# Mixer order in a two-layer hybrid decoder: the third output-gate block is multiplied ahead of the last part of the linear attention

## Chip, cores and metric

The kernel runs on one core of a Trainium2 chip. The metric is the device time in microseconds of one execution, and the number quoted is the median of several runs. Beside the runs there is one execution recorded by the hardware profiler, from which all rows below come. TensorE is called PE here (its weight loads PEld), VectorE DVE, ScalarE ACT, GpSimd POOL, and SyncE, which issues the DMAs, SP.

## What is computed

Two decoder layers over 512 prompt tokens and 8 x 4 sample tokens, width 1024. Each layer has four residual sub-layers:

```
x += 0.5 * SwiGLU_1(rmsnorm(x))
h  = rmsnorm(x);  z = h @ w_in          # one projection, columns split among head groups
     A: sliding-window attention (window 128, 8 query heads, 2 key/value heads, sinks, rotary)
     B: gated linear attention (4 heads, 64 x 128 state), then per head
        o = rms_norm(o, gain) * silu(gate)
x += concat(A, B) @ w_out
x += CrossAttn(rmsnorm(x), memory K/V)
x += 0.5 * SwiGLU_2(rmsnorm(x))
```

The outputs are the new activations, caches and states. The change lies in the second sub-layer, the mixer: `gate` has four heads of 128 columns, and one block of the kernel multiplies one head.

## The kernel before

Activations lie transposed, 128 features by 544 tokens a tile (N = 544, halves of 272). A 1024-deep product of one 128-column block is made in three terms from high and low parts of weights and activations (`product`, L221): 8 x 3 weight tiles times two halves, 48 matmuls on line L230. `weights` (L209) turns a loaded slab (`raw`, three buffers) into `hi` (ACT, L213, three buffers) and `lo` (DVE, L214, two buffers).

The mixer (L679) is written as steps, generators that are cut into parts at each `yield`. The text MIX (L53) names the steps in the order in which their parts are traced; the first mention of a step runs its first part, the next mention its second, and so on (`run`, L72). From this order a planner makes each engine's instruction list: it places an instruction when its inputs and its buffer are there, and prefers what stands earlier in MIX. So an instruction that is late in MIX can come early on its engine when earlier ones can't be placed. On the chip the lists are fixed.

Buffers come from rings: `pm` in PSUM holds two tiles (for a product or for one set of scores), `pa` in PSUM four, `z` six, `s` (scores) five, `u` three.

The steps that matter here:
- `rot i` (L965): a block of the attention's keys (i = 0) or queries. ACT's `taken` (L406) reads the product twice: L409 scales it, L410 squares it into a `u` buffer. The second part rotates it, with four small DMAs into a `z` tile and DVE products L986 to L988.
- `gla n` (L817): the linear attention for 128 tokens. Part one: scores and state updates (L825, L837, L848). Part two: outputs into two `pa` banks (L861, L871). Part three, `normed` (L792): squares L799 and root L803 on ACT, reciprocal L804 and products L807 on DVE into a `z` tile, four transposes L812 on PE, gain L813 on ACT. `glas` does the same for the sample tokens; `states` (L932) makes their new states in four parts (kdm L941 and update L952 on DVE, matmuls L946).
- `qf` (L993): row sums (L272) of the four `u` tiles of the queries, copies L275, transposes L278, then the softmax factors.
- `score n w` (L538): part one multiplies scores into a `pm` tile (L554) and copies them to an `s` tile with the mask (L559/L560, or L564 on ACT and L565 on DVE). Part two: maximum L570, exponentials L576, division L584. Part three: transposes L588 and masks L592. `vals n` multiplies with the values (L604). `swas` does the sample tokens; L619 copies their queries.
- `sv`: the values of the attention, with transposes L1007 to L1011 and 18 small stores.
- `gated h` (L1022): part one takes a `z` tile, multiplies the gate block of head h (48 matmuls) and scales it from PSUM into `z` (L388 on DVE). Part two: silu L1026 on ACT and the product L1027 with the linear attention's output on DVE.
- `bparts` splits the gated outputs into high and low parts; `out half q` multiplies with `w_out` (half 1 takes group B's output, half 0 the attention's).

Of the kernel before, what the change touches and what calls it, by code (L numbers as in the profile page):

```python
# [53 lines left out]
    "rot 0, gate, key 0, query 1, value 2, query 0, key 1, qdecay 1, value 3, kdecay 1, value 3, kdecay 1, kdecay "  # L54
    "0, sv, value 2, value 0, rot 0, kdecay 0, qdecay 0, value 1, value 0, value 1, gla 0, gla 1, glas, gla 0, "
    "gla 1, gla 2, rot 1, gla 0, gla 2, glas, rot 2, gla 1, gated 0, gla 3, rot 2, rot 1, rot 3, gla 2, rot 4, "
    "glas, states, rot 3, gla 3, rot 4, gla 3, qf, qf, score 1 0, states, score 0 0, gated 0, sv, score 1 0, "
# [1454 lines left out]
```

## Time and profile before

| | before |
|---|---|
| median of 3 runs | 2189.59 us (2189.1 to 2192.12) |
| the profiled execution | 2186.67 us |
| its span, first to last instruction | 2184.5 us |
| PE busy | 2161.6 us |
| DVE busy | 1567.0 us |
| ACT busy | 1048.6 us |
| mean granted clock of PE | 0.998 |

Busy time is the time in which at least one instruction of the engine runs. The idle time of an engine is put before the instruction that ended it, with what that instruction waited for. Times in rows are microseconds from the start of the span. The mixer of the first layer lies at about 400 to 620 us, that of the second at about 1480 to 1700 us.

### The profile page before, as it was taken

How to read it: one execution, taken by the hardware profiler on the slowest of the kernel's cores; microseconds unless marked ns; L12 is line 12 of the kernel's file. 1: busy time of each engine (PE TensorE's matmuls, PEld its weight loads, DVE VectorE, ACT ScalarE, POOL GpSimd, SP SyncE). 2: the span in 40 equal slices, each digit the busy share in tenths (PEclk: the TensorE clock that was granted, in tenths of full speed). 3: DMA queues.
4: the chain of work that ended last, by engine and by line, in shares of the span. 5: the costliest groups of instructions: out<-in, count | busy, mean ns of one | idle time of the engine just before them, and what ended most of it. 6: DMA issues, size and time to landing. Idle time of an engine off the chain costs nothing.

```text
span 2184.5 us, 40867 instructions
## 1 busy us (share of the span) xinstructions
PE 2161.6 (99%) x17306; PEld 2088.7 (96%) x17306; DVE 1567.0 (72%) x2471; ACT 1048.6 (48%) x1721; POOL 7.0 (0%) x17
## 2 busy tenths in 40 slices
PE   9999999999999999999999999999999999999999
PEld 9899999997897999999999999999879979999999
DVE  7887876546764798777689777765477458977774
ACT  6444543536455644444364444445455566444441
POOL 0000000000000000000000000000000000000000
PEclk9999999999999999999999999999999999999999
DMA  4233333232335233233232322333223533233332
GB/s 151 89 104 93 113 105 121 88 92 75 96 127 202 78 107 106 87 104 101 68 106 88 107 97 88 101 126 97 77 82 98 190 131 104 94 105 93 87 107 71
DMA packets 74998, 227.07 MB, mean 104 GB/s; under 512 B 7712, under 2 KB 19744, under 8 KB 73504
## 3 DMA queue, kind: packets, MB, share of 16 engines
q1 hardware_dynamic: 74816, 224.47, 32.2%
q8 instruction: 135, 2.21, 0.4%
q14 instruction: 47, 0.39, 0.1%
HBM read 214.64 MB, written 9.04 MB: 102 GB/s over the span
## 4 chain that ended last, share of the span: by engine, by line
PE 94%; DVE 3%; DMA 1%; ACT 1%; issue 0%; SPq 0%; ACTq 0%; DVEq 0%
PE pm L230 47%; PE pa L459 36%; PE pm L1150 1%; PE pm L1112 1%; PE pa L230 1%; DMA raw<-in_wts_dram 1%; PE pm L1235 1%; PE pa L1252 1%; PE pa L604 0%; PE pa L239 0%; PE pm L554 0%; PE pa L1282 0%; PE pa L272 0%; DVE big L219 0%; PE pa L588 0%; DMA out_dram<-state 0%
## 5 line engine op out<-in xcount | busy, mean ns | idle before, releaser
L230 PE MATMUL pm<-big,hi 128*128 128x272 f32 x5632 | 780.5, 290 | 5.7 <-DVE big L316 1.9
L230 PEld LDWEIGHTS pm<-big,hi 128*128 128x128 f32 x5632 | 732.6, 188 | 15.0 <-DVE big L316 2.9
L230 PE MATMUL pm<-big,lo 128*128 128x272 f32 x2816 | 410.1, 289 | 0.0
L230 PEld LDWEIGHTS pm<-big,lo 128*128 128x128 f32 x2816 | 374.1, 188 | 2.2 <-issue 1.2
L213 ACT CAST hi<-raw 128x1024 fp32r<-128x1024 f32 x196 | 205.6, 1049 | 243.4 <-PE pm L230 132.6
L214 DVE TENSOR_TENSOR lo<-raw,hi 128x1024 fp32r<-128x1024 f32 x196 | 238.5, 1217 | 53.9 <-PE pm L230 32.0
L218 ACT CAST hs<-sum 128x1024 fp32r<-128x1024 f32 x152 | 160.0, 1052 | 172.0 <-PE pa L459 122.5
L459 PE MATMUL pa<-t,hs 128*128 128x272 f32 x1368 | 238.9, 288 | 1.3 <-ACT t L218 1.3
L459 PE MATMUL pa<-big,hs 128*128 128x272 f32 x1064 | 211.0, 288 | 2.1 <-DVE big L219 2.1
L459 PEld LDWEIGHTS pa<-t,hs 128*128 128x128 f32 x1368 | 200.9, 188 | 1.5 <-ACT t L218 1.5
L219 DVE TENSOR_TENSOR ls<-sum,hs 128x1024 fp32r<-128x1024 f32 x152 | 185.1, 1218 | 3.3 <-ACT hs L218 2.3
L459 PE MATMUL pa<-big,hi 128*128 128x272 f32 x1216 | 178.5, 289 | 0.0
L399 DVE SCALAR_TENSOR_TENSOR x<-pm,x 128x544 f32<-128x544 f32 x192 | 137.9, 719 | 47.9 <-PE pm L230 47.9
L459 PEld LDWEIGHTS pa<-big,hs 128*128 128x128 f32 x1064 | 166.3, 188 | 2.6 <-DVE big L219 2.6
L459 PEld LDWEIGHTS pa<-big,hi 128*128 128x128 f32 x1216 | 162.9, 188 | 0.0
L459 PE MATMUL pa<-t,ls 128*128 128x272 f32 x912 | 153.1, 289 | 0.0
L459 PEld LDWEIGHTS pa<-t,ls 128*128 128x128 f32 x912 | 129.7, 188 | 0.0
L218 ACT CAST hi<-raw 128x1024 fp32r<-128x1024 f32 x76 | 80.1, 1054 | 84.3 <-PE pm L230 78.2
L218 ACT CAST hd<-raw 128x512 fp32r<-128x512 f32 x76 | 47.2, 621 | 136.1 <-PE pa L459 127.3
L445 DVE TENSOR_TENSOR sum<-raw 128x512 f32<-128x512 f32 x152 | 98.2, 686 | 17.7 <-DMA raw<-in_wts_dram 17.4
L459 PE MATMUL pa<-big,lo 128*128 128x272 f32 x608 | 109.1, 288 | 0.0
L484 DVE TENSOR_TENSOR z<-pa,e 128x272 f32<-128x272 f32 x76 | 33.5, 441 | 98.2 <-PE pa L459 91.8
(306 smaller groups left out, 2675.1 us busy)
## 6 DMA issues: line engine op xcount, KB each, us to landing
raw<-in_wts_dram SPq DMA_DIRECT2D x348, 512.0 KB
big<-in_cmk_t_dram SPq DMA_DIRECT2D x8, 1024.0 KB
big<-in_cmv_dram SPq DMA_DIRECT2D x8, 1024.0 KB
kc<-in_consts_dram SPq DMA_DIRECT2D x2, 1546.0 KB
x<-in_x_dram SPq DMA_DIRECT2D x8, 272.0 KB
z<-big SPq DMA_DIRECT2D x32, 68.0 KB
out_dram<-x SPq DMA_DIRECT2D x8, 272.0 KB
cache<-in_s_dram SPq DMA_DIRECT2D x8, 256.0 KB
```

Source lines behind the costliest of these rows:

```text
L213: act.copy(out=hi, in_=raw)
L214: dve.tensor_tensor(out=lo, in0=raw, in1=hi.bitcast(F32), op=ALU.subtract)
L218: act.copy(out=hi, in_=src)
L219: dve.tensor_tensor(out=lo, in0=src, in1=hi.bitcast(F32), op=ALU.subtract)
L230: pe.matmul(half_of(ps, h, s.stop - s.start), w, x[:, s], start=i == 0, stop=i == len(steps) - 1)
L399: dve.scalar_tensor_tensor(out=x, in0=p, scalar=scale, in1=x, op0=ALU.mult, op1=ALU.add)
L445: dve.tensor_tensor(out=t[:, e], in0=t[:, 0] if x is None else x, in1=y, op=ALU.add)
L459: pe.matmul(ps, u, v, start=first and i == 0, stop=i == len(steps) - 1, skip_group_check=not first)
L484: dve.tensor_tensor(out=t[:, 1], in0=q, in1=e2, op=ALU.add)
L1112: pe.matmul(pk[:, h, :], w[:, o:o + 128], x[:, k, :], start=st and h % 2 == 0, stop=sp and h % 2 == 1)
L1150: pe.matmul(pv[:, c, :], x[:, k, c * 128:c * 128 + 128], w[:, o], start=st, stop=sp)
L1235: pe.matmul(ps[:, h, :], qn[:, h, 128 * n:128 * n + 128], held["mk"][:, h, :], start=True, stop=True)
```

## The change

In MIX, the first mention of `gated 2` moves from behind the third part of `score 1 0` to a place between the second part of `rot 4` and the third part of `gla 3`. The second mention of `gated 2` (silu and product) stays, and so does the order of all other steps. No function is changed. The order of the steps that load weights stays too: `rot 4`, `gated 2`, `gated 1`, `gated 3`.

```diff
-    "glas, states, rot 3, gla 3, rot 4, gla 3, qf, qf, score 1 0, states, score 0 0, gated 0, sv, score 1 0, "
-    "states, score 0 1, score 1 1, score 1 0, gated 2, score 0 0, score 0 1, score 0 0, score 2 0, score 0 1, "
+    "glas, states, rot 3, gla 3, rot 4, gated 2, gla 3, qf, qf, score 1 0, states, score 0 0, gated 0, sv, score 1 0, "
+    "states, score 0 1, score 1 1, score 1 0, score 0 0, score 0 1, score 0 0, score 2 0, score 0 1, "
```

## Rows read from the trace of the kernel before

**Rows 1.** The page's engine table: busy us (share of the span) xinstructions.

```profile
PE 2161.6 (99%) x17306; PEld 2088.7 (96%) x17306; DVE 1567.0 (72%) x2471; ACT 1048.6 (48%) x1721; POOL 7.0 (0%) x17
```

**Rows 2.** Waits of PE, 400 to 620 us: total, times, longest.

```profile
PE pa L812 <- DVE z L807: 2.1, 1, 2.1
PE pa L272 <- ACT u L410: 1.5, 1, 1.5
```

**Rows 3.** Windows, second layer: length, busy us by engine, PE's clock, DMA, GB/s.

```profile
1596.95:1604.19 7.24, 5.09 (x29) 1.99 (x28) 5.95 (x14) 2.71 (x7) 0.00 (x0) 0.76 0.24 75
...
1599.20:1602.50 3.30, 3.30 (x18) 1.02 (x18) 2.94 (x9) 0.70 (x2) 0.00 (x0) 0.50 0.02 5
```

**Rows 4.** Timeline of PE, first layer: start, length, instruction, count, [idle before].

```profile
514.85 1.13 PE L554 MATMUL pm<-kt,big 64*128 64x256 f32 x8
515.91 0.65 PE L946 MATMUL pa<-vgs,kdm 32*64 32x128 f32 x8
518.67 0.30 PE L812 MATMUL pa<-ident,z 128*128 128x128 f32 x1 [2.10 <-DVE z L807]
...
520.58 0.72 PE L554 MATMUL pm<-kt,big 64*128 64x128 f32 x8
522.78 1.10 PE L272 MATMUL pa<-u,kc 128*32 128x272 f32 x4 [1.48 <-ACT u L410]
```

**Rows 5.** Timeline of ACT in the same stretch.

```profile
514.97 0.28 ACT L799 ACTIVATE z<-pa 128x128 f32<-128x128 f32 x1 [1.77 <-PE pa L871]
...
516.15 0.30 ACT L803 ACTIVATE sm<-sm,eps 128x4 f32<-128x4 f32 x1
...
521.47 0.60 ACT L619 COPY qbd<-big 64x128 f32<-64x128 f32 x2 [0.71 <-DVE big L988]
522.10 0.62 ACT L410 ACTIVATE u<-pm 128x544 f32<-128x544 f32 x1
```

**Rows 6.** Timeline of DVE in the same stretch.

```profile
512.22 1.23 DVE L214 TENSOR_TENSOR lo<-raw,hi 128x1024 fp32r<-128x1024 f32 x1 [0.27 <-PE pm L230]
...
516.48 0.18 DVE L804 RECIPROCAL sm<-sm 128x4 f32<-128x4 f32 x1 [2.77 <-ACT sm L803]
...
518.11 0.75 DVE L807 TENSOR_TENSOR z<-pa,sm 128x256 f32<-128x256 f32 x2
```

**Rows 7.** Timelines of PE, ACT and DVE around the block of gated 0.

```profile
491.35 0.45 PE L871 MATMUL pa<-state,big 64*64 64x128 f32 x8
...
494.67 0.69 ACT L813 ACTIVATE big<-pa,col 128x512 f32<-128x512 f32 x1 [6.74 <-PE pa L812]
...
496.36 1.28 ACT L1026 ACT_TABLE_LOAD   x1
498.08 0.66 ACT L1026 ACTIVATE z<-z 128x544 f32<-128x544 f32 x1 [0.44 <-DVE z L388]
498.64 0.26 ACT L799 ACTIVATE z<-pa 128x128 f32<-128x128 f32 x1
...
497.32 0.72 DVE L388 TENSOR_TENSOR z<-pm,r 128x544 f32<-128x544 f32 x1 [9.52 <-PE pm L230]
```

**Rows 8.** Timeline of PE: one undisturbed block.

```profile
429.17 4.19 PE L230 MATMUL pm<-big,hi 128*128 128x272 f32 x32
433.20 2.16 PE L230 MATMUL pm<-big,lo 128*128 128x272 f32 x16
```

**Rows 9.** Timelines of ACT, DVE and PE under the first softmax.

```profile
529.64 1.28 ACT L576 ACT_TABLE_LOAD   x1
530.94 0.49 ACT L576 ACTIVATE s<-s,sm,inv 128x128 f32<-128x128 f32 x1
...
541.90 0.57 ACT L564 COPY s<-pm 128x512 f32<-128x512 f32 x1
...
544.28 0.72 DVE L565 COPY_PREDICATED s<-kc,pm 128x512 f32<-128x512 uint32 x1
...
536.47 0.66 PE L588 MATMUL pa<-ident,s 128*128 128x128 f32 x4
```

## Prediction

> **What bounds the kernel now.** I read the page's engine table first, to see which engine could set the time: PE is busy for 99% of the span [rows 1]. So an edit that adds and removes no work can only gain where PE waits, or lose where it makes PE wait. Next the list of waits of PE inside the first layer's mixer: two waits stand out, 2.10 us and 1.48 us [rows 2, 4]. They sit together, in the order of PE's instructions: after the second part of the linear attention's last step (`gla 3`, done at about 514.9) PE has the scores of `score 1 0` (L554) and eight state matmuls (L946), and then nothing until the transposes L812 of `gla 3`'s third part at 518.67. The second wait stands before the last four row sums L272 at 522.78 [rows 4].
>
> The first wait is a chain on two engines: squares L799 from 514.97, root L803, reciprocal, then two products L807 that end at 518.86 [rows 5, 6]. Its 3.9 us has only 1.06 + 0.6 us of PE work beside it. The row sums can't go earlier: they need `pa` banks, which L807 frees. The second wait is for L410, the squares of `rot 4`: they need a `u` buffer, of which there are three, and which the first twelve L272 free; L410 then stands on ACT behind the copies L619 [rows 5]. No score fills either hole, as both `pm` tiles are held, one by `rot 4` until L410, one by a score.
>
> The second layer has the same stretch. There the first wait was followed by 3.3 us at a granted clock of 0.50, the 1.2 GHz level, so that PE shows busy in place of the second wait; the stretch lasts 7.24 us there and 7.3 us in the first layer (516.56 to 523.88) [rows 3, 4]. So I count the first layer's 3.58 us for each, 7.2 us for both, whether it shows as idle or as slow.
>
> **The change part by part.** The step moved is the first part of `gated 2`: a weight tile, 48 matmuls L230, one L388. No instruction is added. Its second part (silu and product) stays where it is in the text.
>
> *The matmuls.* A whole block takes PE 4.19 + 2.16 us, less 0.16 at each end where neighbours overlap (433.20 against 429.17 + 4.19): 6.03 us [rows 8]. Its weights are ready in the new place: there are two `lo` buffers, so the L214 that starts at 512.22, when `rot 4`'s block has ended, already writes the weights of the gate block after this one [rows 6]. Its output takes a `pm` tile that is free, the one that `score 1 0` took at 514.85. So it runs from about 515.5 (`gla 3` done, plus 0.6 us of L946) to 521.5, over the whole hole. As the order of weight tiles is unchanged, no load is moved; on SP the step passes only the sixteen small stores and two others of `sv`, for which nobody on PE waits. POOL is not passed.
>
> *The wait that it adds.* `score 1 0` now needs the `pm` tile back, from L388 (0.72 us, [rows 7]): 521.5 to 522.3, 0.8 us in which PE may have nothing.
>
> *The normalization of `gla 3`.* Here an order matters that the diff doesn't show. The tile `z` of `gated 2` is now asked for ahead of `gla 3`'s. The trace has this very pair one step earlier: `gla 2`'s outputs were on PSUM at 491.80, ACT was idle until 494.67, and yet their squares L799 came at 498.64, behind L388 and silu of `gated 0`, whose `z` stands ahead in the step order [rows 7]. I read from it that buffers are handed out in step order, though that row fits other reasons too. Then L799 of `gla 3` isn't planned before L388 of `gated 2`. On the chip nothing else holds it, so it starts between 514.97, as now, and about 521.6, where L388 does. At the late end L799 to L807 takes 1.2 + 0.30 + 0.18 + 0.75 and hand-overs [rows 5, 6], 2.5 us without the two rotation products that stood in the chain, and L812 is ready at 524.1. PE meanwhile has `score 1 0` (1.06 us, 522.3 to 523.4). The first wait becomes 0.8 us (chain early) to 1.5 us (late); I take 0.8, as ACT and DVE are nearly empty there.
>
> *The row sums.* L812 and twelve L272 take 1.9 us (518.67 to 520.58, [rows 4]), to about 525.3. L410 follows; L619 no longer stands ahead of it, as its own input is there sooner. `score 0 0` (0.7 us) covers it. If silu of `gated 2` with its table load (0.66 + 1.28, [rows 7]) is put in between, up to 1.0 us is left. I take 0.2.
>
> *The cover given up.* `gated 2` stood under the softmax: the first exponential starts at 530.94, 8.2 us after the last row sums start, and the first transposes L588 at 536.47, 5.5 us later [rows 4, 9]. After the change the last row sums start near 526.1, so L588 may be due at 539.8. From 526.7 PE has the other two scores (2 x 0.72), eleven transposes of the factors and of `sv` (1.7 us, estimated from four L588 in 0.6), four groups of L946 (4 x 0.65), `score 2 0` (1.06) and the block `gated 1` moved up (6.03): 12.8 us, to 539.5. Nearly enough; then `gated 3` moves up in turn, and the output blocks follow. I cost it at 0, with up to 2 us per layer beyond.
>
> **Sum.** Per layer 3.58 - 0.8 - 0.2 = 2.6 us; two layers 5.2 us. The profiled execution took 2186.67 us (2184.5 span and 2.2 around it) and becomes 2181.5. The median of the runs, 2189.59, is 2.9 above that execution; I shift it by the same 5.2 to 2184.4. Ends of this case: both waits gone, 2182.4; 1.5 and 1.0 left, 2187.4.
>
> A rule speaks against it. The table load before the softmax starts 1.28 us before the exponential that it serves at 530.94 [rows 9], so a switch costs 1.3 us by the trace. The Trainium skill (ScalarE: Activation LUTs, What ACT_TABLE_LOAD costs) puts a switch at 1.28 us and a drain of 1.38 us, and advises to finish one set before the next. An early silu would add two switches per layer; were all of it on the path, the sum would be 2189.5 by the row and 2195 by the page. The row shows no such drain.
>
> **Rivals.**
> - *The chain only moves.* ACT takes silu of `gated 2` first, as it did for `gated 0` [rows 7], then needs the square-root table again: 522.3 + 0.66 + 1.2 + 1.28 + 0.30 + 0.18 + 0.75 with hand-overs is 526.7 for L812. PE idles 0.8 + 3.3 = 4.1 us in place of 3.58. For it: the same pair in the trace. Against: when L388 starts, L799 has all its inputs and silu doesn't. 2190.6.
> - *The cover is missed: slower.* `score 2 0` holds a `pm` tile until its copies L564 and L565 are done, at 545.00 now, 14.1 us after the first exponential, since they queue behind all sixteen exponentials [rows 9]. If they do so again, `gated 3` can't start before 534.3 + 14.1 = 548.4, while PE runs out at 539.5 + 1.3 (two L588) + 1.06 (`score 2 1`) = 541.9: 6.5 us of idle, a loss of 3.9 us per layer net, 2197.4. It turns the change into a loss once that copy ends after 541.9 + 2.6 = 544.5. Against: `score 2 0` is now multiplied before the exponentials begin, so its copy can go first.
> - *It hardly shows.* Small waits for `pm` tiles among the scores eat half or more of the gain, or PE's order on the chip comes out nearly as it is: about 2188.5.
>
> **How the numbers follow.** Forecast 0.52, chain moves 0.18, cover missed 0.15, hardly shows 0.15. About 0.2% (4.4 us) is what a measurement can tell from no change. Of the forecast's 0.52 some 0.42 saves more than that; with a little from the rest, faster 0.44. The slow rival and the tail of the first give slower 0.18; same 0.38. The range takes in the ends of the forecast, the chain that moves and the weak gain, and leaves out most of the slow rival: 2182 to 2193.
>
> **What would show it.** Right: a whole run of L230 between L871 and L812 of `gla 3` in both layers, PE's waits in the mixer near 1 us in place of 3.6, and no clock of 0.50 in the second layer there. L799 of `gla 3` behind L388 with silu ahead: the first rival. A wait of several us before a gate block with L565 as its releaser: the second. I am wrong if PE's idle time in the mixer stays where it was, or comes back between 535 and 560.

## Result and the profile after

The change makes the kernel slower: 2202.62 us median (2200.92 to 2204.61) against 2189.98 us for the kernel before in the same comparison, a ratio of 1.0062 with a 95% interval of 1.0052 to 1.0072. The prediction said 2184.4 us, with a range up to 2193.

The profiled execution has a span of 2198.9 us, against 2184.5. First the page's engine table, which answers [rows 1].

```profile
PE 2166.2 (99%) x17306; PEld 2090.3 (95%) x17306; DVE 1566.0 (71%) x2471; ACT 1053.7 (48%) x1725; POOL 7.0 (0%) x17
```

The span grew by 14.4 us. PE's busy time grew by 4.6 us with the same 17306 instructions, so some of them ran slower. Its idle time (span less busy) grew from 22.9 to 32.7 us, by 9.8. ACT has four instructions more, which are table loads, two per layer.

Next the waits of PE in the first layer's mixer, 400 to 620 us (total, times, longest), against [rows 2]. The second layer has the same ones.

```profile
PE pa L812 <- DVE z L807: 3.3, 1, 3.3
PE pm L554 <- DVE s L565: 1.3, 1, 1.3
PE pa L604 <- DVE pt L592: 1.0, 2, 0.7
PE pm L554 <- DVE z L388: 0.8, 1, 0.8
PE pm L230 <- DVE s L565: 0.7, 1, 0.7
PE pm L230 <- DVE x L397: 0.4, 1, 0.4
```

The wait for L807 that the change was to cover is still there and longer, 3.3 in place of 2.1 us. The row sums no longer wait. The 0.8 us for L388 is new, and so are five waits behind 558 us, 3.4 us together, where the kernel before had 0.2: 0.36, 1.27 and 0.70 us at 559 to 565 us, 0.66 at 590 and 0.44 at 605.

The timelines of ACT and PE show the first of these places, against [rows 4, 5].

```profile
521.72 0.28 ACT L799 ACTIVATE z<-pa 128x128 f32<-128x128 f32 x1
...
523.00 1.28 ACT L1026 ACT_TABLE_LOAD   x1
524.30 0.66 ACT L1026 ACTIVATE z<-z 128x544 f32<-128x544 f32 x1
524.97 1.28 ACT L803 ACT_TABLE_LOAD   x1
526.26 0.30 ACT L803 ACTIVATE sm<-sm,eps 128x4 f32<-128x4 f32 x1
```

```profile
522.93 1.13 PE L554 MATMUL pm<-kt,big 64*128 64x256 f32 x8 [0.82 <-DVE z L388]
527.38 0.44 PE L812 MATMUL pa<-ident,z 128*128 128x128 f32 x1 [3.32 <-DVE z L807]
527.75 2.04 PE L272 MATMUL pa<-u,kc 128*32 128x272 f32 x12
```

The squares of `gla 3` start at 521.72, not at 514.97 as before. Between them and their root stand a table load, the silu of `gated 2` and a second table load, 3.2 us in all. The twelve row sums then take 2.04 us (in a kernel below, at the full clock, twelve take 1.12). The windows with a granted clock of 0.50, the 1.2 GHz level, show it (length, busy us of PE, PEld, DVE, ACT and POOL, PE's clock, DMA share, GB/s); the kernel before had one of 3.4 us in its mixers [rows 3], this one has four times that.

```profile
527.27:530.68 3.41, 3.30 (x18) 1.39 (x18) 1.61 (x3) 0.64 (x2) 0.00 (x0) 0.50 0.00 0
564.82:568.23 3.41, 3.41 (x17) 3.41 (x17) 3.39 (x10) 1.05 (x1) 0.00 (x0) 0.50 0.02 5
1612.71:1619.53 6.82, 5.07 (x26) 2.55 (x27) 3.32 (x7) 3.29 (x6) 0.00 (x0) 0.50 0.15 62
```

The second place lies 20 us behind the part that the prediction had followed. The timelines of PE and DVE there:

```profile
562.75 1.13 PE L554 MATMUL pm<-kt,big 64*128 64x256 f32 x8 [1.27 <-DVE s L565]
564.58 1.77 PE L230 MATMUL pm<-big,hi 128*128 128x272 f32 x7 [0.70 <-DVE s L565]
```

```profile
559.57 0.71 DVE L388 TENSOR_TENSOR z<-pm,r 128x544 f32<-128x544 f32 x1
560.20 1.22 DVE L214 TENSOR_TENSOR lo<-raw,hi 128x1024 fp32r<-128x1024 f32 x1
561.33 0.72 DVE L219 TENSOR_TENSOR big<-big 128x544 fp32r<-128x544 f32 x1
561.97 0.72 DVE L565 COPY_PREDICATED s<-kc,pm 128x512 f32<-128x512 uint32 x1
```

All four gate blocks are done by then. A score and an output block want `pm` tiles, and those are emptied by L565, which stands in DVE's queue behind the scaling L388 of the last gate block and two splits (L214, L219). DVE never pauses there, while PE waits.

So there are three possible losses: the chain in front, the cover given up, and the clock behind each wait. The experiments take them one by one.

### The profile page after: what moved, and what is told of

It reads as the page before. It is cut to its first block, busy times and chain, and to the rows that moved or that the text cites. A ratio compares the mean times of both kernels' runs of the same rounds, so it can differ in the third digit from the quotient of the medians.

```text
span 2198.9 us, 40868 instructions
## 1 busy us (share of the span) xinstructions
PE 2166.2 (99%) x17306; PEld 2090.3 (95%) x17306; DVE 1566.0 (71%) x2471; ACT 1053.7 (48%) x1725; POOL 7.0 (0%) x17
## 4 chain that ended last, share of the span: by engine, by line
PE 93%; DVE 4%; ACT 2%; DMA 1%; issue 0%; SPq 0%; ACTq 0%; DVEq 0%
PE pm L230 46%; PE pa L459 36%; PE pm L1150 1%; PE pm L1112 1%; PE pa L230 1%; DMA raw<-in_wts_dram 1%; DVE big L219 1%; PE pm L1235 1%; PE pa L1252 1%; PE pa L604 0%; PE pa L272 0%; PE pa L239 0%; PE pa L1282 0%; PE pa L946 0%; PE pm L554 0%; PE pa L871 0%
## 5 line engine op out<-in xcount | busy, mean ns | idle before, releaser
L213 ACT CAST hi<-raw 128x1024 fp32r<-128x1024 f32 x196 | 205.5, 1049 | 249.3 <-PE pm L230 139.2
L214 DVE TENSOR_TENSOR lo<-raw,hi 128x1024 fp32r<-128x1024 f32 x196 | 238.5, 1217 | 51.0 <-PE pm L230 28.6
L219 DVE TENSOR_TENSOR ls<-sum,hs 128x1024 fp32r<-128x1024 f32 x152 | 185.1, 1218 | 2.8 <-ACT hs L218 1.8
L445 DVE TENSOR_TENSOR sum<-raw 128x512 f32<-128x512 f32 x152 | 98.2, 686 | 14.4 <-DMA raw<-in_wts_dram 14.3
L445 DVE TENSOR_TENSOR sum<-sum,raw 128x512 f32<-128x512 f32 x152 | 103.9, 683 | 0.0
```

What stands on the lines that cost most here:

```text
L213: act.copy(out=hi, in_=raw)
L214: dve.tensor_tensor(out=lo, in0=raw, in1=hi.bitcast(F32), op=ALU.subtract)
L219: dve.tensor_tensor(out=lo, in0=src, in1=hi.bitcast(F32), op=ALU.subtract)
L445: dve.tensor_tensor(out=t[:, e], in0=t[:, 0] if x is None else x, in1=y, op=ALU.add)
```

## Experiments

**The order in which a ring is handed out.** Theory 1: `gla 3`'s squares came late because its `z` tile is handed out after that of `gated 2`. On ACT they stand behind the cast L213 and the copies L619, and start 0.4 us ahead of L388. One kernel takes the tile from another ring, a second swaps the two steps in the text. In the comparison of both, the kernel before took 2188.67 us.

```diff
 own_ring (the changed kernel with)
-            z = tmp("z")[:, 0:T].rearrange("p (i e v) -> p e i v", e=2, i=2)
+            z = tmp(tag)[:, 0:T].rearrange("p (i e v) -> p e i v", e=2, i=2)   # "s" for gla 3
 norm_first (in MIX)
-    ... rot 4, gated 2, gla 3, qf, qf, ...
+    ... rot 4, gla 3, gated 2, qf, qf, ...
```

> The changed kernel, with the z tile of gla 3's normalization taken from the ring `s` (five tiles) instead of `z`; nothing else. Theory 1 (buffers of a ring are handed out in step order, so the squares L799 stood behind L388 of gated 2): the squares start near 515 again instead of 521.7, the root follows at once, no silu and no table load stand between them, L807 is done under the gate block, and PE's wait of 3.3 us before L812 is gone, at most 0.8 us stays before the first score, and the clock of 0.50 behind it (3.4 us per layer) is gone too. That is 3.3 + 1.7 = 5.0 us per layer, 10 in all: 2192.6 if the waits at 559 to 565 us and the half clock behind them stay (they then come from the cover given up), 2184 to 2187 if they go too (they then only came from the late softmax). Rival (the squares stand behind the copy L213, which waits for a buffer that PE frees at 520.1, whatever ring they use): L799 stays after 521 and the time at 2202.6.

> The change with one step swapped: the first part of gated 2 stands right behind the third part of gla 3 in the text instead of ahead of it, so that gla 3's z tile is handed out first and nothing else differs. Theory 1: the order of every engine is the one of the kernel with its own ring, so the time is the same within 1 us; the squares start near 515. If the waits at 559 to 565 us stay: 2192.6; if they go: 2184 to 2187. Rival (the block itself has to stand ahead of the normalization to fill the hole): the block then starts after L812, near 519, PE idles 2 to 3.6 us ahead of it as in the kernel before, and the time is 2190 or more.

Measured: own ring 2185.17 us, ratio 0.9982 (0.9974 to 0.9991); normalization first 2185.42 us, 0.9982 (0.9973 to 0.9990). That is 0.8% less than the changed kernel, from where one tile comes from. PE, ACT and DVE run the same order of instructions in both. ACT in the kernel with the normalization first, and then PE:

```profile
515.95 0.28 ACT L799 ACTIVATE z<-pa 128x128 f32<-128x128 f32 x1 [1.78 <-PE pa L871]
...
517.13 0.30 ACT L803 ACTIVATE sm<-sm,eps 128x4 f32<-128x4 f32 x1
...
522.51 1.28 ACT L1026 ACT_TABLE_LOAD   x1
523.80 0.66 ACT L1026 ACTIVATE z<-z 128x544 f32<-128x544 f32 x1
```

```profile
520.74 2.17 PE L230 MATMUL pm<-big,lo 128*128 128x272 f32 x16
522.75 0.27 PE L812 MATMUL pa<-ident,z 128*128 128x128 f32 x1
522.95 1.10 PE L272 MATMUL pa<-u,kc 128*32 128x272 f32 x8
...
532.51 1.14 PE L554 MATMUL pm<-kt,big 64*128 64x256 f32 x8 [0.37 <-ACT s L559]
535.08 1.15 PE L230 MATMUL pm<-big,hi 128*128 128x272 f32 x7 [1.43 <-DVE s L565]
...
560.09 2.01 PE L230 MATMUL pm<-big,hi 128*128 128x272 f32 x14 [1.26 <-DVE s L565]
563.02 0.52 PE L230 MATMUL pm<-big,hi 128*128 128x272 f32 x2 [0.92 <-DVE big L219]
```

The squares and the root come ahead of the gate block's end, L812 follows the block without a wait, and the whole front is free of idle time: theory 1 holds, its rivals fall. But four waits come up behind it, 0.37 + 1.43 + 1.26 + 0.92 = 3.98 us, more than the 3.58 us that the block now covers. The first two are not the lost cover alone. In this order the silu stands between the root L803 and the root L259 of the softmax factors, and ACT loads a table again before L259, 1.28 us from 530.36, ahead of the copies L559 (531.89); DVE idles 1.81 us for L259, and L565 stands behind that chain. The kernel below has the same load and no wait there, as its copies L559 come ahead of it; no run takes the load alone away. The time fell further than the expectation allowed if such waits stay (2192.6); where it fell is the last question below.

**The two table switches.** Here the tiles stay as in the changed kernel, and only the silu is held behind the root.

```diff
+            with tc.issue_after(held["root"]) if h == 2 else nullcontext():   # held["root"]: L803 of gla 3
                 act.activation(out=z, in_=z, func=AF.Silu)
```

> The changed kernel, with the silu of gated 2 held behind the root L803 of gla 3 on ACT; buffers as in the changed kernel. Theory 1 (the 3.3 us before L812 are the silu and two table switches that slipped between squares and root, 1.28 + 0.66 + 1.28 = 3.22 us): L803 follows the squares at 523.0, L812 is ready near 524.3, PE waits 0.8 us before the score and 0.3 us before L812; if the half clock at 527 to 531 came from the 3.3 us of idle, it is gone as well. 3.0 to 4.7 us per layer: 2193 to 2196.6, with the waits at 559 to 565 us as they are. Rival (the late squares alone are the cause, the switch is hidden): L812 stays near 527 and the time at 2202.6.

Measured: 2192.88 us, ratio 1.0011 (1.0002 to 1.0021). ACT and PE in front, from an execution of 2188.5 us, 4.4 below that median:

```profile
523.78 0.30 ACT L803 ACTIVATE sm<-sm,eps 128x4 f32<-128x4 f32 x1
524.09 1.28 ACT L1026 ACT_TABLE_LOAD   x1
525.38 0.66 ACT L1026 ACTIVATE z<-z 128x544 f32<-128x544 f32 x1
```

```profile
525.46 0.30 PE L812 MATMUL pa<-ident,z 128*128 128x128 f32 x1 [0.64 <-DVE z L807]
525.69 1.12 PE L272 MATMUL pa<-u,kc 128*32 128x272 f32 x12
```

The wait for L807 falls from 3.32 to 0.64 us, near the 0.3 expected, and the row sums run at the full clock. So the prediction's chain with late squares (0.8 us and up to 0.7 more) was sized well; what it lacked is the silu between squares and root. The ratio fell by 0.5%, some 11 us (9.7 between the medians), about twice what the wait lost in two layers (5.4 us): PE's busy time is 2159.3 us on the page, 6.9 less than in the changed kernel. The waits behind 558 us are not less: they are now one of 3.5 us for L565, in the second layer with 1.1 us behind it. Windows over that wait and the 3.4 us after it, in both layers:

```profile
558.58:562.09 3.51, 0.00 (x0) 0.00 (x0) 3.51 (x7) 1.23 (x2) 0.00 (x0) 1.00 0.51 149
562.15:565.56 3.41, 3.41 (x15) 3.41 (x16) 3.41 (x9) 1.23 (x1) 0.00 (x0) 0.50 0.02 5
1639.08:1642.60 3.52, 0.01 (x1) 0.01 (x1) 3.52 (x7) 1.24 (x3) 0.00 (x0) 1.00 0.46 149
1642.65:1646.06 3.41, 3.41 (x27) 3.41 (x28) 3.41 (x9) 1.23 (x1) 0.00 (x0) 1.00 0.00 0
```

While PE waits, DVE is busy for all of it: what ends last there is DVE's queue. And the same wait was followed by a clock of 0.50 in one layer and not in the other.

**What the block was worth where it stood.** Theory 2: the block of `gated 2` was cover. In the kernel before it is cut to 6 of its 48 matmuls; two further kernels go the other way and try to put the remaining gate blocks where PE waits. The kernel before took 2189.3 us beside them.

```diff
 before_thin (the kernel before with)
-            product(ps, nx.terms(hi, lo))
+            product(ps, nx.terms(hi, lo)[:1] if i == 16 else nx.terms(hi, lo))
 cover_early (norm_first with)
-    ... score 0 0, score 2 0, score 0 1, score 1 1, vals 0, swas, gated 1, score 2 1, ...
+    ... score 0 0, gated 1, score 2 0, score 0 1, score 1 1, vals 0, swas, score 2 1, ...
 cover_both (cover_early with)
-    ... gated 2, gated 3, score 3 1, vals 1, ...
+    ... gated 2, score 3 1, gated 3, vals 1, ...
```

> The kernel before, with the block of gated 2 cut from 48 matmuls to 6 (one of its eight input tiles is multiplied; weights, L388, silu and the order of steps stay, so the result of head 2's gate is only a part of the sum). It prices the block as cover in its old place. A block takes 6.03 us, so 42 of 48 matmuls are 5.28 us per layer. Theory 2 (the block was cover under the scores and the softmax; with it gone from there, PE waits some 4 us per layer, as the 0.37 + 1.43 + 1.26 + 0.92 us that are left with the normalization first): it saves only 1 to 2 us per layer, 2185 to 2187 against 2188.7. Rival (the block covered nothing, as the prediction costed it): all 10.6 us are saved, 2178.

> The kernel with the normalization first (gla 3, then gated 2), and the first part of gated 1 moved ahead of score 2 0, so that PE has a gate block where it waits 0.37 and 1.43 us for the copies of score tiles at 532 to 535 us. Theory 2 (these waits are scores queueing for two pm tiles, and a block put between them covers them): both go in each layer, the ones at 559 to 563 us stay: 2185.4 - 2 x 1.8 = 2181.8. Rival (score 2 0 then comes late, and its softmax with it; the waits only move behind): 2185 or more, with a new wait for L592 or L565 after 545 us.

> As the one before, and gated 3's first part also moved behind score 3 1, so that a gate block stands between the last two scores, where PE waits 1.26 and 0.92 us at 559 to 563 us. Theory 2: the second pair of waits goes too: 2185.4 - 2 x 4.0 = 2177.5, faster than the kernel before by 0.5%. Rival (the second pair is DVE's own queue, with splits L219 and maxima ahead of the copies, whatever PE has in hand): it comes back before an output block, 2181 to 2185.

Measured: the thin block 2184.87 us, ratio 0.9976 (0.9966 to 0.9987). Of 10.6 us that PE no longer has to do, 4.4 were saved, a little more than expected. Its waits in the first layer, beside the two old ones:

```profile
PE pm L230 <- DVE lo L214: 2.0, 1, 2.0
PE pm L230 <- DVE s L565: 1.5, 1, 1.5
...
PE pa L604 <- DVE pt L592: 0.9, 1, 0.9
```

The 1.5 us for L565 and the 0.9 us for L592 lie at 547 to 557 us and are the cover that is gone; the second layer has 2.2 us of such waits. The 2.0 us is another matter, a weight tile that isn't split yet at 580 us. So theory 2 holds in kind: the block's old place was not free. Beside the 3.1 us per layer that were not saved, such waits are 2.4 and 2.2 us. The account doesn't close in one profile: the first layer has those 2.0 us as well, and two more stretches at 0.50, from 582.74 and 592.98.

The early `gated 1` took 2187.35 us, 0.9987 (0.9979 to 0.9996), and both moves 2204.31 us, 1.0066 (1.0053 to 1.0079), against 0.9982 without them. The expectations of theory 2 fail. The rival of the first kernel holds; for the second neither side has the time. The first can't be told from the kernel without the move by the time alone, as the intervals overlap. With `gated 1` early the waits at 532 to 535 us shrink to 0.4, and PE waits 0.5 and 1.7 us behind 543 us (for L388 and L592) instead. With both moves PE waits once for long, here in its timeline:

```profile
567.99 1.09 PE L588 MATMUL pa<-ident,s 128*128 128x128 f32 x4 [5.04 <-ACT sm L650]
```

Behind it the clock is at 0.50 for 6.8 us, in both layers. The rows can be read so: what PE runs short of isn't a block at one point. From the factors to the first output block, ACT and DVE have a fixed amount of softmax to do in a row, and PE's work beside it has to be spread over all of it. The order of the kernel before does that with 0.2 us of waits; each of the orders tried that takes a block forward pays behind.

**The clock, and where the kernel with the normalization first gains.** Three more kernels ran beside 2189.11 us for the kernel before.

```diff
 after_filled (the changed kernel with, ahead of the root L803)
+            ps = psa().rearrange("p (h t) -> p h t", h=4)
+            for h in range(fill):           # fill = 10 for gla 3, else 0
+                pe.transpose(ps[:, h % 4, :], z[:, h % 2, h // 2 % 2, :], ident)
```

> The changed kernel with ten more transposes (0.22 us each) of gla 3's squared tile into the bank that L812 overwrites, so that PE has something to do in part of the 3.3 us before L812; nobody reads them. The chain on ACT and DVE (squares, silu, two table loads, root, L807) is as in the changed kernel. It prices the clock. Theory 3 (in the changed kernel the row sums behind the 3.3 us run at a clock of 0.50 for 3.4 us, a loss of 1.7 us per layer that was in no term of the sum): L812 is still ready near 527.4, but no clock of 0.50 follows, L278 comes 1.7 us sooner per layer, and the time is near 2199. Rival (the fall has another cause than PE's idle time): the clock still falls at 527 to 531, 2202 to 2204.

> The kernel with the normalization first (gla 3, then gated 2) once more, for a second profile and a second interval. In the first profile PE idles 3.98 us per layer in the mixer, against 3.58 and 0.20 in the kernel before (2.15 in the second layer, with a clock of 0.50 behind it), so by PE's idle time alone it should be no faster than before; it measured 0.9982. Theory 3 (the rest is the clock: it falls behind one wait of 2.1 us, and not behind two of 1.8 and 2.2 that have work between): again no clock of 0.50 in the mixers, 0.997 to 0.999. Rival (the gain was chance): 0.9995 or more, or falls in both kernels alike.

> The kernel before itself, for a second profile: does the clock fall behind the 2.1 us wait for L807 in the first layer, in the second, in both or in none? In the first profile it fell in the second layer alone. Theory 3: at least one fall of 3.4 us again. Rival: none, so that the falls of the kernel before are rare and price nothing. Ratio 1.000.

Measured: filled 2196.43 us, 1.0028 (1.0018 to 1.0038); normalization first again 2185.87 us, 0.9984 (0.9975 to 0.9993); the kernel before again 2189.14 us, 1.0000 (0.9991 to 1.0008).

The filled kernel doesn't price the clock cleanly, and its time lies below both expectations. The transposes also changed PE's order (row sums and scores moved among them), its longest wait there is 2.1 us, before a score, and the clock still fell behind it in the first layer, not in the second. It also fell at its waits of 1.9 us at 563 and 1645 us. Its page gives 2167.1 us of PE busy and a span of 2191.3, so 24.2 of idle, where the changed kernel has 32.7. The ten added transposes take 1.6 us per layer in the trace (not 2.2 as the expectation had it); without them PE's busy time is 2.3 us below the changed kernel's. So filling the wait gave back more than it took, but how much of that is the clock stays open.

The second profile of the kernel before has two falls of the clock in its mixers, where the first had one. Windows:

```profile
520.32:523.73 3.41, 3.41 (x18) 1.14 (x20) 3.41 (x10) 1.15 (x3) 0.00 (x0) 0.50 0.00 1
1602.34:1605.76 3.42, 3.42 (x18) 1.47 (x12) 3.28 (x7) 2.67 (x6) 0.00 (x0) 0.50 0.00 0
```

So behind the 2.1 us wait for L807 the clock fell in three of four cases (in four of six with the thin kernel, whose front is the same), and at the 1.43 us wait of the kernels with the normalization first (three profiles with the own ring's, two layers) in two of six. That none would fall there, as expected, was missed, while the ratio came again.

The mixers themselves are not faster. From L926, just ahead of the changed place, to the first L1112, the first product of the cross-attention's keys, it takes 107.84 and 106.78 us in the kernel before, 107.93 and 106.88 in its second profile; with the normalization first 107.19 and 107.17, then 108.60 and 107.15, and with the own ring 108.68 and 107.18. On average that is 0.3 us per layer more, not less. What the profiles show of the gain lies behind the mixer: from the first L1252 (the cross-attention's first product with the values) to the next layer's L907 it is 887.9 us in both profiles of the kernel before and in the changed one, and 886.25 in all three profiles of the other order, 1.65 us less each time (886.2 with the silu behind the root, too). All waits of PE in that stretch, the kernel before and then the one with the normalization first:

```profile
PE pa L1252 <- ACT pt L1181: 0.4, 1, 0.4
PE pa L1282 <- ACT pt L1181: 0.4, 1, 0.4
PE pm L230 <- ACT big L218: 0.3, 1, 0.3
PE pm L230 <- DVE x L397: 0.2, 1, 0.2
PE pm L230 <- DVE big L219: 0.2, 1, 0.2
```

```profile
PE pa L1282 <- ACT pt L1181: 0.4, 1, 0.4
PE pm L230 <- DVE x L397: 0.2, 1, 0.2
```

These are 0.9 us of the 1.65; the rest is PE's busy time, with the same matmuls. The text of the cross-attention is the same in both kernels, but in the trace its instructions stand in another order on PE: the order is planned from the whole program, and a swap in the mixer moved it. No run moves that order alone, so that this is part of the gain is read from the rows, not shown by an experiment. It is also less than half of the 3.2 to 3.9 us by which the version with the normalization first beats the kernel before (0.16 to 0.18%). Behind the second layer's mixer the profiles differ by 0.5 and 1.0 us, and the own ring's is longer there; where the rest of the gain lies stays open. No profile shows that it comes from what the change is about.

## Why the prediction was wrong, step by step

- *What bounds the kernel, and the two holes:* right. PE's idle time (9.8 us) and slower instructions (4.6 us) make up the whole difference of 14.4.
- *The matmuls:* right. The block runs over the hole, and the row sums don't wait any more.
- *The wait that it adds:* right, 0.82 us for L388 against 0.8.
- *The normalization of `gla 3`:* half right. The squares come at the late end that was named (521.72 against 521.6), and for the reason named, the order in which `z` tiles are handed out (with own ring or normalization first they start near 515 again). The step that failed is "L812 is ready at 524.1": silu and two table switches, 3.2 us, went in between squares and root, and it was 527.38. The price of this was the first rival's, 4.1 us of idle; measured are 0.82 + 3.32 = 4.14. That it fits so well is in part luck: the rival had the silu ahead of the squares and one table load on the path, and in fact the squares come first and two loads follow; L812 and the score ahead of it come 0.7 and 0.6 us later than it said. Its argument against, that silu has no input yet when the squares start, was true of the squares but not of the root: the root is due when the fourth square ends (522.98), and L388 ends at 522.87. So the argument didn't rule the case out, and it was given 0.18.
- *The row sums:* 0 against 0.2.
- *The cover given up:* wrong. Costed at 0 with up to 2 us per layer, it is 3.4 us in the changed kernel, and 3.98 with the front repaired. The count of PE's work ran from 526.7 to 539.8 us and stopped at the first transposes L588. In the changed kernel no wait comes there, but with the front repaired, as the forecast had it, 1.8 of the 3.98 us do. And with two gate blocks left under the softmax in place of three, the last one ends too early: 2.3 us of waits come at 559 to 565 us, ahead of the first output blocks, and 1.1 us at 590 and 605. The text named that ("the output blocks follow") and counted no work for it.
- *The clock:* there was no term for it, though [rows 3] showed 3.3 us at 0.50 behind the second layer's wait. It is 4.6 us here by PE's busy time; by half of the time at 0.50 in the mixers (13.6 us against 3.4, or 6.8 in the second profile of the kernel before) it is 5.1 or 3.4.
- *The rivals:* the third one's small waits for `pm` tiles among the scores are there, 1.27 us here and 1.8 us with the front repaired. The second one's mechanism didn't occur. The copy of `score 2 0` came ahead of the exponentials, as its "against" said; on ACT:

```profile
536.84 0.59 ACT L564 COPY s<-pm 128x512 f32<-128x512 f32 x1 [0.28 <-PE pm L554]
...
538.99 0.50 ACT L576 ACTIVATE s<-s,sm,inv 128x128 f32<-128x128 f32 x1
```

- *The rule on tables:* it was right to speak against the forecast; both switches lay on the path. Holding the silu behind the root took 2.7 us off the wait. That agrees with the Trainium skill (ScalarE: Activation LUTs, Table sets: the hidden batching unit), which says to batch activation calls by set. Of the drain that the Trainium skill puts beside a load (ScalarE: Activation LUTs, What ACT_TABLE_LOAD costs) no row here shows anything: the last square ends at 522.98, the load starts at 523.00 and lasts 1.28 us, and silu starts at 524.30.
- *The range:* each case stood alone in it. The first rival, a missed cover and the clock came together, and their sum is what was measured: idle in front 8.3 us for both layers in place of 5.7 (the second layer's row sums show no wait before, as they run slow there), 6.9 us behind in place of 0.4, and 4.6 to 5 us of clock, some 14 us in these two profiles.

## What to carry to other kernels

A step moved ahead in a written order takes its buffers ahead too: look which later step now gets its tile second, and what slips in between the parts of that step on its engine. A block of work that hides one wait may be hiding another where it stands; to price it, follow the engine's work up to the point where the last such block is used up, not only to the next wait. And price a wait with the clock behind it, as the rows of the same kernel show it, in more than one profile.

## Not expected of the hardware

Behind a wait of 2.1 us PE's granted clock fell to 0.50 for 3.4 us in four of six cases, at one of 1.43 us in two of six, and behind 3.5 us in one of two, each in the same code. Not every fall stands behind a wait: the one at 592.98 in the thin kernel comes 10.5 us after PE's last wait. So one wait can cost 1.7 us (half of 3.4) more in one layer or execution than in another, and one profile of each kernel can't tell orders apart whose waits differ by less.
